# A transformer layer on one Trainium2 core: the dilated heads are placed between the NSA heads, and the order's estimate counts transfers and the port that VectorE and GpSimd share

## Chip, cores and metric

The kernel runs on one core of a Trainium2 chip. The metric is device time in microseconds (us) for one execution of the whole layer. Before the change it is 1748.33 us, the median of three runs (1747.14, 1748.33 and 1748.94 us).

## What is computed

One decoder layer on 1024 tokens of width 1024, in float32: a normalisation, one input projection, three causal token mixers side by side, a gated merge, a residual, and a gated feed-forward network with a short convolution. Cut to what matters here:

```python
h = rms_norm(x, norm1_g)
proj = h @ w_in + b_in                      # 6166 columns: q, k, v of all heads, and 3 x 1024 gate columns
y_a = fox_attention(qa, ka, va, fa)         # 4 heads, full causal, a decay per head
y_b = dilated_attention(qb, kb, vb, ...)    # 6 heads in 3 groups, strides 1, 4, 16; outputs weighted by their
                                            # softmax denominators
y_c = nsa_attention(qc, ...)                # 6 heads in 2 groups; each head has three parts:
#   scores against 63 compressed keys -> probabilities p_c and, summed over the group's three heads, an importance
#   of 16 blocks of 64 tokens; the 8 best blocks are selected for each query
#   "selected" attention over those blocks, and "window" attention over the last 512 tokens
g = sigmoid(gates).reshape(1024, 3, 1024)
merged = g[:, 0] * (y_a @ w_pa) + g[:, 1] * (y_b @ w_pb) + g[:, 2] * (y_c @ w_pc)
x = x + merged @ w_o
x = x + conv_ffn(rms_norm(x, norm2_g), ...)
out = rms_norm(x, final_g)
```

The compressed scores of a group must be known before its selected heads can start; its window heads do not need them. The 24 gate blocks (128 gate columns each, numbered 0 to 23) are needed only in the merge.

## The kernel before, in words

**Arithmetic.** Every float32 operand is split into a high and a low float32r part: ScalarE (ACT) casts the high part and VectorE (DVE) or GpSimd (POOL) subtracts to get the low one. A product is then three matmuls on TensorE (PE): high by high, high by low, low by high (`mm3`, L285 to L287).

**Stages.** (1) Normalisation, transposes, the first token projection, gate blocks 0 and 1, and the sums of tokens that the next stage needs (`token_sums`, L473 to L490). Gate blocks 0 and 1 are made by `gate` (L1436): a tile `f4` is filled by ACT in two halves, and each half is stored by a transfer on ACT's queue (L1440). The tag `f4` has two buffers, and `token_sums` takes its working tiles from the same two. (2) `proj_pairs` (L545 on) makes two blocks of 128 output columns at a time from seven half-size products in place of eight, 84 matmuls of 512 columns for a pair; 18 blocks of q, k and v and then the gate blocks 18 to 23 (`PAIRED = 18`), twelve pairs. (3) The compressed keys and values. (4) Attention, about 400 to 866 us in the trace. (5) Loads of the three mixers' outputs (`branch`, L1514 to L1519), the gate blocks that are left, and the merge. (6) Output projection. (7) Feed-forward network. The feed-forward and everything behind attention is not edited.

**Attention's order.** Attention is written as generators (one for each head, each strip of scores, each transpose, each product, each split). `Flow` runs them against an estimate: a queue for each of PE, DVE, ACT and POOL, a cost in us and a level for each request. When an engine is free in the estimate, the request of the lowest level is emitted. So `Flow` sets the program order on PE, DVE and ACT, and with it the order in which SyncE (SP) issues the transfers; on the chip each engine then works through its own list in that order. `yield "DVE", 1, 0.66, f` asks for DVE for 0.66 us at level 1. `F.move(kb)` is the estimate of a transfer, at 200 GB/s after all transfers that were already counted.

**What a head does.** `strips` computes the scores of two rows of 128 queries (L805 to L809, PE, level 2); `soften` takes the row maximum (DVE, L833) and the exponential (ACT, L841); the factors 1/sum follow (DVE, L850 to L853); `norm` multiplies the probabilities by them, on DVE (L864) or ACT (L865), whichever is free first in the estimate. The probabilities are transposed on PE (L907, level 1) into one of three PSUM banks X0 to X2, split by ACT (L923) and DVE (L926), and multiplied with the values (L953, L954, level 0). ACT and DVE take the result out (L970, L974) and SP stores it (L979). q, k and v tiles have two buffers each; a head's loads are issued when a buffer of its kind comes free.

**The order of the heads before.** A table `ORDER` of four kinds: f is a FoX head, d a dilated head, w a window head, n a selected head, and s, one for each NSA group, is the compressed scores of its three heads (L1329 to L1332, then DVE L1352 to L1377) and the selection (`nsa_rows`, L1391 to L1421). An s loads the q tiles of all three heads only for this. The w and n heads load them again.

**The filler.** Gate blocks from 3 up are made during attention by `fill`, one matmul at a time at level 9 (L1465): a block is 48 matmuls of 512 columns in two halves of 24, which sit in the banks X0 to X2 as well. The next block's weights are split meanwhile (`next_split`: ACT L1489, then one POOL instruction over 128x1024, L1493). `gate_out` adds the bias on ACT (L1476) into the tile `f4`, [128, 1024], one buffer in this stage, and SP stores each half (L1479). Thirteen blocks, 3 to 15, are filled; 16 and 17 are made behind attention, where `branch` loads too.

Of the kernel before, what the change touches and what calls it, by code (L numbers as in the profile page):

```python
# [6 lines left out]
F32 = mybir.dt.float32  # L7
# [8 lines left out]
P = 128  # L16
S = 1024
# [124 lines left out]
class Flow:  # L142
# [7 lines left out]
    def __init__(self):  # L150
        self.now, self.moved, self.n, self.events = 0.0, 0.0, 0, []
# [7 lines left out]
        self.groups, self.turned = r(), r()  # L159
# [14 lines left out]
    def step(self, g, value):  # L174
# [16 lines left out]
        else:  # L191

            taken = []
            for e, level, cost, emit, *lat in ask if isinstance(ask, list) else [ask]:
                self.n += 1
                heapq.heappush(self.queues[e], (level, self.n, cost, emit, lat[0] if lat else self.LAT[e], g, taken))
# [6 lines left out]
    def run(self):  # L203
        while True:
            while self.events and self.events[0][0] <= self.now + 1e-9:
                heapq.heappop(self.events)[2]()
            for e, q in self.queues.items():
                while q and q[0][6]:
                    heapq.heappop(q)
                if q and self.free[e] <= self.now + 1e-9:  # L210
                    _, _, cost, emit, lat, g, taken = heapq.heappop(q)
                    taken.append(e)
                    out = emit()
                    self.free[e] = self.now + cost
                    self.at(self.free[e] + lat, lambda g=g, out=out: self.step(g, out))
                    self.at(self.free[e], lambda: None)
# [5 lines left out]
class Trunk:  # L222
    def __init__(self, tc, a, taps=None):
# [4 lines left out]
        self.psA, self.steps = None, None  # L228

# [138 lines left out]
    def constants2(self):  # L368
# [39 lines left out]
        self.k2c = t([114, 256], F32R, "k2c")  # L408
# [131 lines left out]
    PAIRED = 18  # L540
# [280 lines left out]
    def soften(self, pair, part, ps, bank, place):  # L821
# [33 lines left out]
        yield "DVE", 0, 0.26 if pair.gates is None else 0.39, factors  # L855
# [5 lines left out]
    def norm(self, pair, x, left):  # L861
        nc, F = self.nc, self.F
        p, f, n = pair.blocks[x], pair.sm[:, 6 + x:7 + x], (pair.rows[x][2] - pair.rows[x][1] + 1) * P
        yield [("DVE", 1, 0.13 + n * 0.47e-3, lambda: nc.vector.tensor_scalar(p, p, f, None, ALU.mult)),  # L864
               ("ACT", 3, 0.16 + n * 0.85e-3, lambda: nc.scalar.mul(p, p, f))]  # L865
# [132 lines left out]
    def attention(self):  # L998
# [20 lines left out]
        def free(kind, n=1):  # L1019
# [10 lines left out]
                "s": lambda g: [head(set(), [lambda h=h: self.load_q(c, h, 6 + h)])[0] for h in range(3 * g, 3 * g + 3)],  # L1030
# [50 lines left out]
        pcs = {}  # L1081

        def select(g):
            pcs[g] = yield from self.nsa_select(g, heads["s", g], lambda: free("q"))

        def group_head(kind, h):
# [3 lines left out]
            k, v = heads[kind, 3 * g][1:]  # L1090
            vc = self.Box(t=self.vcs[g, 0 if r == 0 else 1], ready=Mark())
            vc.ready.on = True
            c0 = 0 if r == 0 else (r - 1) * 64
            for ip in range(4):
# [12 lines left out]
                if kind == "n":  # L1107
                    pc, ready = pcs[g]
                    self.t_step(u, [[(x, lambda i=i, c0=c0: pc[:, i, c0:c0 + P]) for x, i in enumerate((a, b))]],
# [984 lines left out]
```

## Time and profile before

| what | value |
|---|---|
| runs | 1747.14, 1748.33, 1748.94 us |
| the profiled execution's own time | 1745.82 us |
| its span, first to last instruction | 1744.1 us, 24501 instructions |
| mean clock granted to TensorE | 0.988 |
| PE busy | 1661.0 us (95%) |
| DVE busy | 1313.2 us (75%) |
| ACT busy | 830.5 us (48%) |
| POOL busy | 469.1 us (27%) |
| transfers | 275 MB, 158 GB/s on average |

The profiled execution is 2.5 us below the median of the runs. A busy PE in this profile is not PE at its peak: matmuls are pipelined, so that a 512-column matmul is shown with 0.39 us while the next one starts after 0.23 us. Times on the left of a row of the timeline are us from the span's start; what stands in square brackets behind a row is how long the engine had been idle before it, and what it had waited for.

### The profile page before, as it was taken

How to read it: one execution, taken by the hardware profiler on the slowest of the kernel's cores; microseconds unless marked ns; L12 is line 12 of the kernel's file. 1: busy time of each engine (PE TensorE's matmuls, PEld its weight loads, DVE VectorE, ACT ScalarE, POOL GpSimd, SP SyncE). 2: the span in 40 equal slices, each digit the busy share in tenths (PEclk: the TensorE clock that was granted, in tenths of full speed). 3: DMA queues.
4: the chain of work that ended last, by engine and by line, in shares of the span. 5: the costliest groups of instructions: out<-in, count | busy, mean ns of one | idle time of the engine just before them, and what ended most of it. 6: DMA issues, size and time to landing. Idle time of an engine off the chain costs nothing.

```text
span 1744.1 us, 24501 instructions
## 1 busy us (share of the span) xinstructions
PE 1661.0 (95%) x8468; PEld 1379.2 (79%) x8468; DVE 1313.2 (75%) x2230; ACT 830.5 (48%) x1599; POOL 469.1 (27%) x332
## 2 busy tenths in 40 slices
PE   6889999999989899999989999899999999999998
PEld 6678888877878688888877788688887888888876
DVE  8846776565886799888467617999999999866764
ACT  5323443235846378878555413433333343454451
POOL 3742322211010000000114320655546544200000
PEclk9999999999998999999999999999999999999999
DMA  6445566377776665332176710144545454487661
GB/s 205 119 128 145 151 167 167 122 177 184 199 209 175 171 203 160 101 112 64 54 256 203 269 49 13 37 163 157 188 149 195 163 170 157 140 269 230 213 228 51
DMA packets 228267, 275.08 MB, mean 158 GB/s; under 512 B 21412, under 2 KB 162314, under 8 KB 227934
## 3 DMA queue, kind: packets, MB, share of 16 engines
q1 hardware_dynamic: 224958, 265.48, 50.7%
q10 hardware_dynamic: 2736, 5.24, 0.8%
q0 software_dynamic: 448, 2.78, 0.5%
q8 instruction: 67, 1.10, 0.3%
q14 instruction: 58, 0.48, 0.1%
HBM read 194.23 MB, written 81.93 MB: 158 GB/s over the span
## 4 chain that ended last, share of the span: by engine, by line
PE 57%; DVE 20%; DMA 7%; issue 6%; ACT 5%; POOL 4%; SPq 0%; POOLq 0%; DVEq 0%; ACTq 0%
PE X L1465 6%; PE dn L287 5%; PE dn L285 5%; PE dn L286 5%; PE S L286 4%; PE S L287 4%; PE S L285 4%; PE X L907 3%; PE T L287 3%; DVE t L1730 3%; PE T L286 3%; PE T L285 3%; PE PV L954 2%; PE S L809 2%; DVE u L1788 2%
## 5 line engine op out<-in xcount | busy, mean ns | idle before, releaser
L926 DVE TENSOR_TENSOR tl<-X,th 128x512 fp32r<-128x512 f32 (+2 forms) x202 | 116.5, 586 | 24.9 <-ACT th L923 22.9
L1493 POOL TENSOR_TENSOR wl<-wr,wh 128x1024 fp32r<-128x1024 f32 x13 | 31.1, 2389 | 347.2 <-ACT wh L1489 314.0
L923 ACT CAST th<-X 128x512 fp32r<-128x512 f32 (+2 forms) x202 | 101.1, 507 | 39.6 <-PE X L907 36.0
L907 PE MATMUL X<-ident,p 128*128 128x128 f32 x610 | 99.4, 278 | 4.4 <-DVE tl L926 1.7
L833 DVE TENSOR_REDUCE sm<-S 128x1 f32<-128x640 f32 (+7 forms) x128 | 87.7, 711 | 20.0 <-PE S L809 19.7
L1730 DVE SCALAR_TENSOR_TENSOR t<-u,ccols,t 128x511 f32<-128x511 f32 (+1 forms) x88 | 96.7, 1099 | 7.5 <-ACT t L1725 6.4
L841 ACT ACTIVATE p<-S,sm 128x640 f32<-128x640 f32 (+7 forms) x128 | 90.9, 715 | 16.6 <-DVE sm L833 15.9
L953 PE MATMUL PV<-th,v 128*128 128x256 f32 (+1 forms) x362 | 94.6, 283 | 0.7 <-DVE y L974 0.7
L809 PE MATMUL S<-k,q 98*128 98x128 f32 (+6 forms) x240 | 91.7, 390 | 3.5 <-DMA q<-dq_c 2.5
L954 PE MATMUL PV<-tl,v 128*128 128x256 f32 (+1 forms) x362 | 90.0, 282 | 1.9 <-DVE tl L926 1.8
L805 PE MATMUL S<-k,q 128*128 128x512 f32 (+2 forms) x240 | 83.0, 346 | 7.1 <-ACT p L841 7.1
L1465 PE MATMUL X<-hTh,wl 128*128 128x512 f32 x208 | 86.5, 416 | 0.0
L1465 PE MATMUL X<-hTl,wh 128*128 128x512 f32 x208 | 86.3, 415 | 0.0
L1465 PE MATMUL X<-hTh,wh 128*128 128x512 f32 x208 | 85.5, 411 | 0.4 <-ACT f L1476 0.4
L907 PEld LDWEIGHTS X<-ident,p 128*128 128x128 f32 x610 | 70.9, 142 | 13.9 <-DVE tl L926 3.2
L263 POOL TENSOR_TENSOR wl<-wr,wh 128x384 fp32r<-128x384 f32 (+2 forms) x31 | 44.2, 1425 | 126.2 <-ACT wh L261 92.6
L954 PEld LDWEIGHTS PV<-tl,v 128*128 128x128 f32 x362 | 69.2, 191 | 6.7 <-DVE tl L926 3.2
L953 PEld LDWEIGHTS PV<-th,v 128*128 128x128 f32 x362 | 69.2, 191 | 3.6 <-ACT th L923 1.1
L1655 POOL TENSOR_TENSOR su<-wr 128x512 f32<-128x512 f32 x20 | 31.0, 1549 | 144.5 <-DMA wr<-w_up 71.3
L285 PE MATMUL dn<-hTh,wh 128*128 128x512 f32 x148 | 60.0, 405 | 10.2 <-ACT f L1436 10.2
L1731 ACT ACTIVATE t<-t 128x512 f32<-128x512 f32 x44 | 27.9, 633 | 82.6 <-DVE t L1730 82.6
L287 PE MATMUL dn<-blk,wh 128*128 128x512 f32 x152 | 60.4, 398 | 1.9 <-POOL wh L1667 1.0
(815 smaller groups left out, 5568.7 us busy)
## 6 DMA issues: line engine op xcount, KB each, us to landing
wr<-w_up SPq DMA_DIRECT2D x66, 256.0 KB
gr<-dg SPq DMA_DIRECT2D x24, 512.0 KB
t<-w_down SPq DMA_DIRECT2D x22, 512.0 KB
dt<-t SPq DMA_DIRECT2D x22, 512.0 KB
wr<-w_in SPq DMA_DIRECT2D x20, 512.0 KB
wr<-dl SPq DMA_DIRECT2D x39, 256.0 KB
wr<-w_in SPq DMA_DIRECT2D x36, 256.0 KB
q<-dq_c SPq DMA_DIRECT2D x18, 512.0 KB
```

Source lines behind the costliest of these rows:

```text
L285: nc.tensor.matmul(out, st[0], mv[0], start=first, stop=False)
L286: nc.tensor.matmul(out, st[0], mv[1], start=False, stop=False)
L287: nc.tensor.matmul(out, st[1], mv[0], start=False, stop=last)
L809: nc.tensor.matmul(out, q.t[1][0:R, qs], k.t[1][0:R, cs], start=False, stop=True)
L841: nc.scalar.activation(o.rearrange("p a b -> p (a b)"), u, AF.Exp, bias=mx[:, x:x + 1], accum_out=sm[:, 2 + x:3 + x])
L907: nc.tensor.transpose(ps[:, n * P:(n + 1) * P], b(), self.ident)
L923: nc.scalar.copy(g.th[:, cs], ps[:, cs])
L926: yield "DVE", 0, 0.07 + cs.stop * 1.04e-3, lambda: nc.vector.tensor_tensor(g.tl[:, cs], ps[:, cs], g.th[:, cs].bitcast(F32), ALU.subtract)
L953: nc.tensor.matmul(unit.pv[:, oc], w, g.th[:, cs], start=first and i == 0, stop=False)
L954: nc.tensor.matmul(unit.pv[:, oc], w, g.tl[:, cs], start=False, stop=e)
L1465: nc.tensor.matmul(p, w[i][:, k], self.hT[hh][j][:, k], start=x == 0, stop=x == 23)
L1730: nc.vector.scalar_tensor_tensor(o, i, cw[2 - sh], o, ALU.mult, ALU.add)
```

## The change

It has six parts.

1. **The order of the heads.** The kind s is gone. `nsa_select` is called at the start of each window head, with that head's own q tile, for its two halves; after the group's third window head the selection `nsa_rows` runs. `ORDER` has 22 heads in place of 24, and the six dilated heads stand between the NSA heads of group 0 (w0 d0 w1 d1 w2 d2 n0 d3 n1 d4 n2 d5), the FoX heads 1 to 3 between the window heads of group 1 (w3 f1 w4 f2 w5 f3), and n3 n4 n5 at the end as before. The second part of the compressed keys `k2c` has 98 rows in place of 114, since a window head's q tile has no rows for the selection; those rows were zero.
2. **The shared port in the estimate.** Requests are now either `DVE` or `DVE*`; `DVE*` (the factors, `norm`, the sums of the compressed scores, the selection, the dilated merge) and `POOL` do not run at the same time in the estimate. A request that waits for the port is passed over by others. Some costs were changed (`norm`, the selection).
3. **Splits in pieces.** The POOL instruction L1493 over 128x1024 becomes four over 128x256, with 0.65 us each in the estimate.
4. **Transfers in the estimate.** The stores of gate blocks and the loads of their weights are counted with `F.move`. The weights' load is issued before that wait rather than 2 us after the split.
5. **The gate tile.** `f4`, [128, 1024], becomes two tiles of [128, 512], `f0` and `f1`, in attention and behind it, taken in turn by each half; a half's tile comes free in the estimate when its store has landed. In the first stage both halves take a tile of 512 from the tag `f4`.
6. **Eight gate blocks in pairs.** `PAIRED` is 16: the blocks 16 to 23 are made in pairs, thirteen pairs in all; `fill` makes 3 to 13; 14 and 15 are made behind attention.

From L285 on, line numbers are 12 to 15 higher in the new code, and from L1326 on 5 to 15 higher.

```diff
@@ class Flow
+        self.f, self.groups, self.turned = r("f0", "f1"), r(), r()
...
+                port, e = e in ("DVE*", "POOL"), e.rstrip("*")
+                heapq.heappush(self.queues[e], (level, self.n, cost, emit, lat[0] if lat else self.LAT[e], g, taken, port))
...
+                ready = [o for o in q if not o[6] and not (o[7] and self.port > self.now + 1e-9)]
...
+                op = min(ready, key=lambda o: o[:2])
...
+                if port:
+                    self.port = self.free[e]
@@ proj_pairs
-    PAIRED = 18
+    PAIRED = 16
@@ norm
-        yield [("DVE", 1, 0.13 + n * 0.47e-3, lambda: nc.vector.tensor_scalar(p, p, f, None, ALU.mult)),
-               ("ACT", 3, 0.16 + n * 0.85e-3, lambda: nc.scalar.mul(p, p, f))]
+        yield [("DVE*", 1, 0.13 + n * 0.5e-3, lambda: nc.vector.tensor_scalar(p, p, f, None, ALU.mult)),
+               ("ACT", 3, 0.2 + n * 0.85e-3, lambda: nc.scalar.mul(p, p, f))]
@@ attention
-                "s": lambda g: [head(set(), [lambda h=h: self.load_q(c, h, 6 + h)])[0] for h in range(3 * g, 3 * g + 3)],
...
+            if kind == "w":
+                if r == 0:
+                    sels[g] = self.Box(pc=self.ap.tile([P, NT, 192], F32, "pc"), done=Mark(),
+                                       imp=self.ap.tile([P, 4, 64], F32, "imp"))
+                    sels[g].done.on = True
+                yield from self.nsa_select(g, r, q, sels[g])
+                if r == 2:
+                    F.proc(self.nsa_rows(g, sels[g]))
...
-    ORDER = (("f", 0), ("d", 0), ("d", 1), ("f", 1), ("d", 2), ("d", 3), ("s", 0), ("f", 2), ("d", 4), ("d", 5),
...
+    ORDER = (("f", 0), ("w", 0), ("d", 0), ("w", 1), ("d", 1), ("w", 2), ("d", 2), ("n", 0), ("d", 3), ("n", 1), ("d", 4),
...
@@ gate
-        gt = self.st.tile([P, S], F32, "f4")
...
+            gt = self.st.tile([P, 512], F32, self.gate_tags[hh])
@@ fill
-        for f in range(3, self.PAIRED):
+        for f in range(3, self.PAIRED - 2):
...
-            F.proc(self.next_split())
+            if self.wloaded:
+                F.proc(self.next_split())
@@ gate_out
+        place = yield F.f
+
+        def out():
+            gt = self.ap.tile([P, 512], F32, place)
+            nc.scalar.activation(gt, ps, AF.Identity, bias=self.cols[:, 20 + f:21 + f])
+            return gt
+
+        gt = yield "ACT", 0, 0.6, out
         F.dn.give(bank)
         yield 0.1
-        nc.sync.dma_start(self.dg[f][:, cs], gt[:, cs])
+        nc.sync.dma_start(self.dg[f][:, cs], gt)
+        yield F.move(256)
+        F.f.give(place)
@@ next_split
-        yield "POOL", 0, 2.4, low
+        for k in range(0, 8, 2):
+            yield "POOL", 0, 0.65, lambda k=k: low(k), 0.0 if k < 6 else F.LAT["POOL"]
         mark.set(F)
-        yield 2.0
         self.load_w()
+        yield F.move(512)
```

Three places in the programs show what moves. The first is SP's queue where the last loads before group 1 of the NSA heads are issued, before the change; `dg<-f` is the store of half a gate block, and what stands ahead of it are loads of q, k and v.

```order
L775 DMA v_5808<-dv_a_150 128x8x128
L754 DMA q_1049_5875<-dq_c_145 128x1024
L755 DMA q_1050_5876<-dq_c_145 64x1024
L758 DMA q_1050_5876<-dax_30_135 34x1024
L766 DMA k_1051_5880<-dk_w_149 64x1024
L767 DMA k_1051_5880<-dk_w_149 64x1024
L768 DMA k_1052_5881<-dk_w_149 64x1024
L770 DMA k_1052_5881<-day_141 34x1024
L775 DMA v_5886<-dv_w_153 128x8x128
L1479 DMA dg_165<-f_1031_5754 128x512
```

This is the same queue in the changed program where the keys of the second window group are loaded.

```order
L991 DMA dyb_59_164<-y_1211_6533 64x256
L770 DMA q_1223_6579<-dax_33_138 34x1024
L787 DMA v_6576<-dv_b_151 128x8x128
L778 DMA k_1224_6583<-dk_w_149 64x1024
L779 DMA k_1224_6583<-dk_w_149 64x1024
L780 DMA k_1225_6584<-dk_w_149 64x1024
L782 DMA k_1225_6584<-day_141 34x1024
L991 DMA dyb_59_164<-y_1216_6555 64x256
L1489 DMA dg_165<-f_1229_6611 128x512
```

Before, two values tiles, a q and a k stand in one block ahead of the gate's store; now the loads of q, v and k are spread between stores of outputs.

The second place is DVE in the compressed scores of the first group, before the change: `csm` and `ce` are the sums and the exponentials, `imp` the importance, `pc` the probabilities.

```order
L1352 TENSOR_REDUCE csm_4902<-S_845_4843 128x4
L1353 TENSOR_SCALAR csm_4902<-csm_4902 128x4
L1354 TENSOR_TENSOR ce_4901<-S_845_4843,csm_4902 128x256
L1363 TENSOR_REDUCE csm_4902<-ce_4901 128x4
L1364 TENSOR_SCALAR csm_4902<-csm_4902 128x4
L1365 RECIPROCAL csm_4902<-csm_4902 128x4
L1372 TENSOR_TENSOR imp_4748<-ce_4901,csm_4902 128x256
L1373 TENSOR_TENSOR pc_4747<-imp_4748,gsig_396 128x4x64
L974 TENSOR_TENSOR y_858_4931<-PV_4908,y_858_4931 64x256
L1352 TENSOR_REDUCE csm_4955<-S_853_4888 128x4
```

And this is the same second half of a head's compressed scores in the changed program, inside the window head 0.

```order
L1357 TENSOR_REDUCE csm_4014<-S_639_3952 128x4
L1358 TENSOR_SCALAR csm_4014<-csm_4014 128x4
L1359 TENSOR_TENSOR ce_4013<-S_639_3952,csm_4014 128x256
L938 TENSOR_TENSOR tl_650_4011<-X_646_3996,th_649_4010 128x512
L986 TENSOR_TENSOR y_654_4028<-PV_3975,y_654_4028 64x256
L1368 TENSOR_REDUCE csm_4014<-ce_4013 128x4
L1369 TENSOR_SCALAR csm_4014<-csm_4014 128x4
L1370 RECIPROCAL csm_4014<-csm_4014 128x4
L1377 TENSOR_TENSOR imp_3898<-ce_4013,csm_4014 128x256
L1378 TENSOR_TENSOR pc_3897<-imp_3898,gsig_396 128x4x64
L938 TENSOR_TENSOR tl_658_4042<-X_653_4023,th_657_4041 128x512
```

The wait of DVE for ACT's exponential, between `ce` and the next `csm`, now has other heads' splits (`tl`) and outputs (`y`) in it, and the next head's compressed scores no longer follow at once.

The third place is ACT in the first stage, around the second half of gate block 0, before the change. `f_149` is a working tile of the token sums, `f_150` the gate tile, and `T3h` and `T4h` are casts of the sums.

```order
L588 CAST wh_899<-wr_893 128x512
L1436 ACTIVATE f_150_696<-dn_748,cols_364 128x512
L588 CAST wl_902<-wr_893 128x512
L1440 DMA dg_165<-f_150_696 128x512
L473 CAST T4h_476<-sl_775 128x512
L473 CAST T3h_474<-f_149_690 128x512
L473 CAST T4h_476<-f_149_690 128x512
L1436 ACTIVATE f_168_811<-dn_812,cols_364 128x512
```

Here is the same place in the changed program, where `f_159` is the second half's own tile.

```order
L600 CAST wh_901<-wr_895 128x512
L485 CAST T3h_474<-f_149_690 128x512
L485 CAST T4h_476<-f_149_690 128x512
L1441 ACTIVATE f_159_773<-dn_748,cols_364 128x512
L485 CAST T4h_476<-sl_776 128x512
L1445 DMA dg_165<-f_159_773 128x512
L600 CAST wl_904<-wr_895 128x512
L1441 ACTIVATE f_170_837<-dn_812,cols_364 128x512
```

Two casts of `f_149` have moved ahead of the gate's second half.

More of the change, by code (lines that the diff above doesn't have):

```diff
@@ L207, in run @@
             for e, q in self.queues.items():
[L208 to L216, printed above, removed]
+                if not q or self.free[e] > self.now + 1e-9:
+                    continue
+                ready = [o for o in q if not o[6] and not (o[7] and self.port > self.now + 1e-9)]
+                q[:] = [o for o in q if not o[6]]
+                heapq.heapify(q)
+                if not ready:
+                    continue
+                op = min(ready, key=lambda o: o[:2])
+                q.remove(op)
+                heapq.heapify(q)
+                _, _, cost, emit, lat, g, taken, port = op
+                taken.append(e)
+                out = emit()
+                self.free[e] = self.now + cost
+                if port:
+                    self.port = self.free[e]
+                self.at(self.free[e] + lat, lambda g=g, out=out: self.step(g, out))
+                self.at(self.free[e], lambda: None)
             if not self.events:
@@ L1079, in dil_head @@
             free("k")
-        pcs = {}
-        def select(g):
-            pcs[g] = yield from self.nsa_select(g, heads["s", g], lambda: free("q"))
+        sels = {}
         def group_head(kind, h):
@@ L1186, in below @@
                 nc.vector.tensor_tensor(ln[:, g], ln[:, g], mx, ALU.subtract)
-        yield "DVE", 3, 0.7, below
+        yield "DVE*", 3, 0.7, below
         yield "ACT", 3, 1.5, lambda: nc.scalar.activation(ln, ln, AF.Exp)
@@ L1377, in rest, with nsa_rows @@
                 nc.vector.tensor_tensor(pd, e, bc(gt), ALU.mult)
-        yield "DVE", 1, 1.4 + 0.6 * half, rest
+        yield "DVE*", 1, 1.4 + 0.6 * half, rest
         F.ce.give()
         done.set(F)
-    def nsa_rows(self, g, imp, before):
-        nc, ap, F = self.nc, self.ap, self.F
-        yield before
+    def nsa_rows(self, g, sel):
+        nc, ap, F, imp = self.nc, self.ap, self.F, sel.imp
+        yield sel.done
         def select():
@@ L1991, in run @@
         gp = Pool(self, "gp", {"gr": 3, "acc": 2})
-        self.st = Pool(self, "last", {"gr": 3, "f4": 2}, side="right")
+        self.st = Pool(self, "last", {"gr": 3, "f0": 2, "f1": 2}, side="right")
         ys = {}
```

100 lines of the change are left out of this document (43 added, 57 removed).

## The prediction

> **What bounds the kernel now.** The windows of the attention stage come first, since most of the edits lie there: length, then the busy time (and instructions) of PE, PE's weight loads, DVE, ACT and POOL, then TensorE's granted clock, the transfers' share and GB/s.
>
> ```profile
> 400.00:866.00 466.00, 442.44 (x2921) 376.24 (x2921) 365.96 (x935) 322.23 (x776) 34.35 (x19) 0.98 0.54 146
> 400.00:480.00 80.00, 77.83 (x516) 65.98 (x516) 56.36 (x146) 57.47 (x148) 7.55 (x5) 1.00 0.73 183
> 480.00:620.00 140.00, 124.69 (x760) 105.31 (x759) 104.69 (x312) 72.82 (x191) 14.34 (x8) 0.93 0.70 186
> 620.00:840.00 220.00, 213.92 (x1491) 182.14 (x1490) 195.10 (x459) 179.53 (x416) 10.00 (x5) 1.00 0.41 120
> 480.00:500.00 20.00, 17.41 (x120) 15.39 (x118) 14.95 (x42) 12.48 (x37) 2.36 (x1) 0.91 0.68 185
> 540.00:560.00 20.00, 17.52 (x114) 16.19 (x112) 11.98 (x39) 12.78 (x47) 0.95 (x1) 0.83 0.53 166
> 600.00:620.00 20.00, 20.00 (x115) 16.62 (x115) 17.08 (x43) 14.85 (x35) 1.97 (x1) 0.87 0.54 121
> ```
>
> PE bounds the stage, but not evenly. It is idle for 466.0 - 442.4 = 23.6 us, and a clock of 0.98 costs another 0.02 x 466 = 9.3 us: 33 us are lost. Of the idle time 140.0 - 124.7 = 15.3 us lie between 480 and 620, where the compressed scores of both groups stand, and there the clock is 0.93. Between 620 and 840, with window and selected heads alone, PE is idle for 6.1 us of 220 (2.8%) at full clock, although DVE is busy there for 89%. So the chip can run this mix with DVE nearly full and PE almost always fed.
>
> The timeline of PE, DVE, POOL, SP and ACT then says what the idle time waits for; the bracket is the idle time before a row.
>
> ```profile
> 494.70 0.41 PE L907 MATMUL X<-ident,p 128*128 128x128 f32 x2 [1.62 <-DVE p L864]
> 522.65 0.60 PE L1408 MATMUL X<-ident,s 128*16 128x128 f32 x4 [2.15 <-DVE s L1398]
> 548.89 0.30 PE L809 MATMUL S<-k,q 98*128 98x128 f32 x1 [2.48 <-DMA q<-dq_c]
> 592.73 0.60 PE L1408 MATMUL X<-ident,s 128*16 128x128 f32 x4 [2.43 <-DVE s L1398]
> 599.58 0.79 PE L805 MATMUL S<-k,q 128*128 128x512 f32 x1 [5.32 <-ACT p L841]
> 622.86 0.39 PE L954 MATMUL PV<-tl,v 128*128 128x256 f32 x1 [1.13 <-DVE tl L926]
> 765.23 0.66 PE L907 MATMUL X<-ident,p 128*128 128x128 f32 x4 [1.68 <-DVE tl L926]
> ...
> 518.28 2.44 DVE L1394 TENSOR_TENSOR sc<-sc,sab 128x64 f32<-128x64 f32 x1
> 761.39 3.19 DVE L864 TENSOR_SCALAR p<-p,sm 128x640 f32<-128x640 f32 x2
> ...
> 518.25 2.39 POOL L1493 TENSOR_TENSOR wl<-wr,wh 128x1024 fp32r<-128x1024 f32 x1 [11.17 <-ACT wh L1489]
> 761.37 2.40 POOL L1493 TENSOR_TENSOR wl<-wr,wh 128x1024 fp32r<-128x1024 f32 x1 [44.51 <-ACT wh L1489]
> ...
> 584.92 6.20 SPq L1479 DMA_DIRECT2D dg<-f  x1
> 598.03 0.69 ACT L1476 ACTIVATE f<-X,cols 128x512 f32<-128x512 f32 x1 [12.30 <-DMA dg<-f]
> ```
>
> Three causes can be read. The longest gap, 5.32 us, belongs to the single gate tile: SP took 6.2 us to issue the store behind a run of q, k and v loads, ACT stood 12.3 us at L1476 until the tile was free, and the exponentials behind it on ACT's list came late. The gap of 2.48 us is a late q. The others are the port: a DVE instruction over 128x64 took 2.44 us beside a POOL split of 2.39 us, and the same happens at 761; PE's gaps of 1.62, 2.15, 1.13 and 1.68 us follow such collisions, 6.6 us in all.
>
> **The change, part by part.**
>
> *One more pair, two filled blocks fewer.* The copy of a pair's first product (L617) appears once in a pair, twelve times; the first and the last row give the period, and one row of the chain of waits gives the price of a filled block of 48 matmuls. A wait of a store stands before the last row, on ACT; PE was busy throughout.
>
> ```profile
> 119.26 0.59 ACT L617 COPY p<-dn 128x512 f32<-128x512 f32 x1 [0.75 <-PE dn L287]
> ...
> 333.58 0.59 ACT L617 COPY p<-S 128x512 f32<-128x512 f32 x1 [2.10 <-DMA dg<-u]
> ...
> 401.45 10.98 PE X L1465 x48
> ```
>
> A pair costs (333.58 - 119.26) / 11 = 19.5 us, all on the path. Two blocks of filler cost 2 x 10.98 = 22.0 us, and attention is bound by PE, so they come off it. Net -2.5 us. If PE did not bound attention any more, their removal would be worth nothing and the pair would be a loss of 19.5 us; that is a rival below.
>
> *The first stage.* PE's gaps around the two gate blocks and the second token projection are these; the two rows of ACT are the gate's second half and the cast that moves ahead of it, those of POOL two steps of the token sums.
>
> ```profile
> 74.90 0.79 PE L285 MATMUL dn<-hTh,wh 128*128 128x512 f32 x1 [5.73 <-ACT f L1436]
> 84.66 0.39 PE L285 MATMUL dn<-bh,hTh 128*128 128x274 f32 x1 [1.81 <-ACT f L1436]
> 98.68 0.39 PE L285 MATMUL dn<-bh,hTh 128*128 128x274 f32 x1 [3.46 <-DVE tm L680]
> ...
> 74.17 0.68 ACT L1436 ACTIVATE f<-dn,cols 128x512 f32<-128x512 f32 x1
> 83.40 0.62 ACT L473 CAST T4h<-f 128x512 fp32r<-128x512 f32 x1 [2.22 <-POOL f L489]
> 70.88 1.71 POOL L487 TENSOR_TENSOR sl<-hTh,sh 128x512 f32<-128x512 f32 x1
> 78.22 1.76 POOL L487 TENSOR_TENSOR f<-hTh,f 128x512 f32<-128x512 f32 x1 [2.90 <-DMA dg<-f]
> ```
>
> Now the working tile `f` waits until both halves of gate block 0 are stored (POOL at 78.22). In the changed order it needs only the first half's store, so it can follow POOL's step at 70.88 directly, at 72.6, 5.6 us earlier; but ACT takes its two casts before the gate's second half. The casts would end at about 83.40 + 0.62 - 5.6 = 78.4 and the second half follow there instead of at 74.2, so the gap of 5.73 grows by about 4 us; the 1.81 behind it and most of the 3.46 should go, and what follows starts earlier, since the next round of sums begins 5.6 us earlier and `tm` on DVE, on which PE waits at 98.68, stands behind it. An estimate from these rows is -2.5 us, with 0 and -4 as ends.
>
> *The compressed scores inside the window heads.* No computation is added: as many instructions on PE, DVE and ACT, and six q loads fewer. What goes is the run of six compressed scores in a row, a chain from DVE to ACT and back in which only the filler keeps PE busy, and the q loads of heads that only this run used. *The gate tile in halves* gives ACT a second tile, so that a store may take the time of a whole half more before ACT stands. *Pieces and the estimate of the port*: the loss at one collision is at most a piece, which costs 2.39 / 4 = 0.6 us by the row above, in place of 2.4. There are four pieces for a block and eleven blocks, 44 instructions in place of 12 or 13; the order avoids collisions only where the chip keeps to the estimate.
>
> What is lost afterwards is the largest unknown, and no row of before shows it. From one side it is bounded by the 33 us of now (the order may move the gaps and remove none), from the other by the part of 620 to 840 that is not a collision, (6.1 - 1.13 - 1.68) / 220 = 1.5%. The work of PE without gaps and at full clock is 466 - 33 - 22 = 411 us: at 1.5% that is 6 us. I take the whole share of 620 to 840, 2.8% of 411 = 11.4 us, and 3.6 us for the clock, two windows like the one at 480 (20 x 0.09 each): 15 us. The mix is the nearest one: DVE's 366 us, less 9 us for four collisions of about 2.2, over 411 + 15 us make 84%, and 620 to 840 ran with 89%. So -18 us, with ends of -27 and 0.
>
> How the clock falls matters for the 3.6 us. In the windows it stood at 0.91 at 480 and at 0.83 at 540, where the gaps were 1.62 and 2.48 us. The Trainium skill, in "TensorE: Matmul & The Clock Gate", Part 1, says that the clock halves only after an idle window of about 3.4 us. This trace differs: shorter gaps were followed by a slower clock. By the page, short gaps would cost no clock, and the sum would be 3.6 us lower.
>
> *Behind attention.* Two blocks are made there as before. SP issues the loads of `branch` behind the last filler's store in both orders, so the gap before the second of these blocks, 3.39 us, stays.
>
> ```profile
> 884.66 0.50 PE L285 MATMUL dn<-hTh,wh 128*128 128x512 f32 x1 [3.39 <-ACT f L1436]
> ```
>
> **The sum** is -2.5 - 2.5 - 18 = -23 us against the profiled execution's 1745.8 us, 1722.8 us. That execution is 2.5 us below the median of the runs, so the forecast for the median is 1725 us.
>
> **The rivals.**
>
> *The pieces do not help.* The chip drifts from the estimate within a few heads. A POOL piece waits for DVE too, and the next block's weights come after four such waits instead of one; POOL's pieces then collide as often as now and the filler is late when a gap needs it. For it: a split that starts a microsecond early or late meets another DVE instruction than the estimate had in mind. Against it: POOL was busy for 34 of 466 us, and a block's split can begin when the block before it begins. It would keep the 6.6 us of collisions and two more windows of clock like the one at 480, 3.6 us: 1725 + 10 = 1735 us.
>
> *Late transfers take the place of the gaps.* The NSA group holds one of two k and one of two v buffers for three heads, so each dilated head's k can only be loaded when the dilated head before it is done, during one window head. A late load costs what the one at 548.89 cost: 2.48 us, and 0.17 x 20 = 3.4 us of clock behind it, 5.9 us. There are nine such changes in the two interleaved groups. Against it: a head between them gives such a load about 18 us (the twelve window and selected heads take the 220 us from 620 on), and the six q loads that go make transfers lighter. If three or four of nine are late, the 18 us are gone: 1746 us, no change that can be measured.
>
> *DVE sets the pace: slower.* With two blocks fewer there is less filler to cover DVE's chains. If DVE reaches only the share that it has now over the whole stage, 366 / 466 = 78.5%, attention takes (366 - 9) / 0.785 = 455 us in place of 466. That is 11 us less against 19.5 more for the pair, and 2.5 less in the first stage: +6, 1754 us. It decides as soon as DVE's share stays under 79.5% (357 / 0.795 = 449; the 17 us saved there and the first stage just pay for the pair). Against it: the 89% of 620 to 840.
>
> **How the numbers follow.** Forecast 0.64, rival of the pieces 0.15, late transfers 0.12, DVE 0.09. About 0.2%, 3.5 us, is what a measurement of this kernel can tell from no change. The forecast and the first rival lie wholly on the faster side (0.79); of the late transfers a quarter is still faster (0.03), the rest within 0.2% (0.09); of the DVE case 0.01 is within 0.2%, the rest slower (0.08). So 0.82, 0.10 and 0.08. The forecast's own range goes from 1725 - 9 - 1.5 - 2.5 = 1712 (gaps of 6 us at full clock, the first stage at -4, and runs that lie no higher than the profiled execution) to 1734 with half of the 18 us; the range reaches on over the rival of the pieces to the edge of the late transfers, 1712 to 1745.
>
> **What would show it.** In the changed kernel's trace: 13 copies L629 (now L617) at 19.5 us; 528 filler matmuls in place of 624; attention's PE idle and slow clock near 15 us in place of 33, and the stage some 40 us shorter (466 - 22 - 18); no ACT wait of 12 us at the gate's bias; no DVE instruction of 128x64 over 1 us in the selection; the gap at 74.90 grown, the one at 98.68 shrunk. The forecast is wrong if gaps at the first scores of dilated heads name a DMA, or if PE's gaps name DVE between all heads while DVE's share stays near 79%.

## The result and the profile after

The changed kernel takes 1717.98 us, the median of four runs (1716.85 to 1719.81), beside 1747.74 us for the kernel before, measured with it. The medians differ by 29.8 us; the ratio is 0.9839, with a 95% interval of 0.9811 to 0.9866, so the kernel is 1.6% faster. The forecast was 1725 us in a range of 1712 to 1745. The profiled execution has a span of 1717.0 us, 27.1 us less than the 1744.1 of before. The other 2.7 us of the medians' difference lie in which execution was profiled: 1.9 us below its median before, 0.9 us above it now.

The stages come first, cut at the same events in both programs: the first pair's copy, the first filler matmul, the end of attention's last matmul, and 95 us of what follows. The columns are those of the prediction's windows: the stretch and its length, the busy time of PE, PE's weight loads, DVE, ACT and POOL with the number of instructions, the granted clock, the transfers' share and GB/s. Before:

```profile
0.00:119.26 119.26, 91.02 (x564) 82.26 (x565) 84.51 (x163) 49.65 (x97) 65.72 (x62) 0.96 0.51 151
119.26:401.26 282.00, 276.28 (x1273) 228.67 (x1271) 187.00 (x264) 105.65 (x168) 82.56 (x58) 1.00 0.59 158
401.26:864.95 463.69, 440.65 (x2912) 374.88 (x2912) 365.53 (x934) 321.18 (x775) 34.28 (x18) 0.98 0.54 146
864.95:960.00 95.05, 87.29 (x367) 68.83 (x367) 60.08 (x73) 47.49 (x63) 29.36 (x22) 0.98 0.68 225
```

And after:

```profile
0.00:117.31 117.31, 89.46 (x564) 81.25 (x565) 88.75 (x163) 49.66 (x98) 65.86 (x62) 0.96 0.51 153
117.31:418.34 301.03, 295.66 (x1356) 244.48 (x1355) 194.64 (x278) 110.89 (x176) 90.38 (x65) 1.00 0.58 155
418.34:837.60 419.26, 412.44 (x2815) 349.89 (x2814) 352.40 (x924) 322.57 (x779) 35.11 (x46) 1.00 0.54 142
837.60:932.90 95.30, 89.03 (x377) 69.61 (x378) 64.19 (x77) 49.53 (x65) 29.20 (x23) 1.00 0.70 232
```

First stage -1.95 us, pairs +19.0, attention -44.4, behind it +0.2: together -27.1. In attention PE now idles for 419.26 - 412.44 = 6.8 us and its clock is 1.00; before it was 23.0 us and 0.98. DVE is busy for 352.4 / 419.3 = 84%.

The three windows that the prediction showed at 480, 540 and 600 us read like this in the changed kernel, though other heads run in them now; all run at full clock, and PE is busy for 58.2 of the 60 us, where it was 54.9:

```profile
480.00:500.00 20.00, 19.82 (x134) 16.14 (x134) 18.19 (x50) 15.66 (x40) 2.98 (x4) 1.00 0.56 158
540.00:560.00 20.00, 18.43 (x125) 15.46 (x123) 17.45 (x49) 16.06 (x42) 0.00 (x0) 1.00 0.88 209
600.00:620.00 20.00, 20.00 (x138) 16.91 (x136) 16.57 (x46) 17.59 (x43) 2.82 (x4) 1.00 0.70 171
```

PE's timeline after, with every gap over 0.8 us from 70 us to the merge, without the pairs and the compressed keys:

```profile
78.74 0.80 PE L297 MATMUL dn<-hTh,wh 128*128 128x512 f32 x1 [9.57 <-ACT f L1441]
98.24 0.39 PE L297 MATMUL dn<-bh,hTh 128*128 128x274 f32 x1 [2.28 <-DVE tm L692]
433.44 0.50 PE L817 MATMUL S<-k,q 128*128 128x512 f32 x1 [1.04 <-ACT p L853]
558.20 0.30 PE L821 MATMUL S<-k,q 98*128 98x128 f32 x1 [1.49 <-issue]
764.01 0.63 PE L919 MATMUL X<-ident,p 128*128 128x128 f32 x4 [0.83 <-DVE tl L938]
839.14 0.50 PE L297 MATMUL dn<-hTh,wh 128*128 128x512 f32 x1 [1.55 <-ACT f L1483]
```

Inside attention three gaps of over 0.8 us are left, none over 1.5 us. ACT's wait of 12.30 us for a gate store has no successor. The longest gap of the kernel, 9.57 us, is the first stage's, in front of gate block 1.

### The profile page after: what moved, and what is told of

Read it like the earlier page. It is cut to its first block, busy times and chain, and to the rows that moved or that the text cites. A ratio compares the mean times of both kernels' runs of the same rounds, so it can differ in the third digit from the quotient of the medians.

```text
span 1717.0 us, 24504 instructions
## 1 busy us (share of the span) xinstructions
PE 1651.3 (96%) x8456; PEld 1367.6 (80%) x8456; DVE 1312.1 (76%) x2234; ACT 837.5 (49%) x1611; POOL 477.3 (28%) x367
## 4 chain that ended last, share of the span: by engine, by line
PE 51%; DVE 25%; issue 8%; DMA 7%; ACT 4%; POOL 4%; SPq 1%; POOLq 0%; DVEq 0%; ACTq 0%
PE X L1470 5%; PE dn L297 4%; PE dn L298 4%; PE dn L299 4%; DVE t L1744 4%; PE X L919 3%; PE S L298 3%; PE S L299 3%; PE S L297 3%; DVE u L1802 3%; PE T L299 2%; PE T L298 2%; PE T L297 2%; PE PV L966 2%; PE S L821 2%
## 5 line engine op out<-in xcount | busy, mean ns | idle before, releaser
L1506 POOL TENSOR_TENSOR wl<-wr,wh 128x256 fp32r<-128x256 f32 x44 | 32.5, 771 | 311.9 <-ACT wh L1501 297.2
L853 ACT ACTIVATE p<-S,sm 128x640 f32<-128x640 f32 (+7 forms) x128 | 90.8, 714 | 14.6 <-DVE sm L845 13.9
L1470 PE MATMUL X<-hTh,wh 128*128 128x512 f32 x176 | 73.1, 415 | 0.0
L1470 PE MATMUL X<-hTh,wl 128*128 128x512 f32 x176 | 72.6, 413 | 0.0
L1470 PE MATMUL X<-hTl,wh 128*128 128x512 f32 x176 | 71.8, 408 | 0.0
L1739 ACT ACTIVATE t<-u,ccols 128x512 f32<-128x512 f32 x44 | 36.0, 817 | 52.2 <-DVE u L1802 49.0
```

The costliest lines, as they stand in the source:

```text
L853: nc.scalar.activation(o.rearrange("p a b -> p (a b)"), u, AF.Exp, bias=mx[:, x:x + 1], accum_out=sm[:, 2 + x:3 + x])
L1470: nc.tensor.matmul(p, w[i][:, k], self.hT[hh][j][:, k], start=x == 0, stop=x == 23)
```

## The experiments

My theory of the gain was that three causes, each removed by its own edit, made the gaps: the gate store, the port and the late q. The rival was that the order of the heads, which spreads DVE's work and the loads, had removed all of them. Each ratio in the table is to the kernel before, run beside it. Attention's length, between the same events, is the finer measure: the same attention program took 419.26, 418.96, 418.50 and 418.19 us in four profiles, while all that lies behind it took between 875 and 882 us in profiles that make two gate blocks there. It still rests on one profile of each kernel.

| kernel | attention, us | PE idle in it | clock | ratio to before, 95% interval |
|---|---|---|---|---|
| changed kernel | 419.3 | 6.8 | 1.00 | 0.9839 [0.9811, 0.9866] |
| changed kernel, again | 419.0 | 6.3 | 1.00 | 0.9847 [0.9820, 0.9874] |
| one gate tile | 417.9 | 5.3 | 1.00 | 0.9856 [0.9832, 0.9881] |
| one POOL piece | 418.7 | 7.4 | 1.00 | 0.9865 [0.9845, 0.9886] |
| no port in the estimate | 419.7 | 8.9 | 1.00 | 0.9868 [0.9845, 0.9890] |
| tile, pieces, port and costs undone | 423.6 | 10.8 | 0.99 | 0.9856 [0.9835, 0.9878] |
| compressed scores in runs | 422.2 | 9.7 | 0.99 | 0.9864 [0.9837, 0.9891] |
| old order of heads | 451.4 | 23.4 | 0.97 | 1.0028 [1.0013, 1.0044] |
| before, new order alone (12 filled blocks) | 440.6 | 13.3 | 0.98 | 0.9896 [0.9857, 0.9936] |
| before, eight gates in pairs alone | 442.0 | 26.3 | 0.99 | 0.9996 [0.9974, 1.0019] |
| changed kernel, ten gates in pairs | 406.9 | 14.6 | 1.00 | 0.9864 [0.9836, 0.9891] |

### One gate tile

```diff
-        place = yield F.f
...
-            gt = self.ap.tile([P, 512], F32, place)
...
+                if gt is None:
+                    gt = self.ap.tile([P, S], F32, "f4")
```

> The changed kernel, with the filler's gate rows again in one tile of 128x1024 that the estimate does not know (attention alone; the gate block before it uses a whole tile too). Theory of three causes (store, port, late q; each edit removes its own): a store behind loads on SP holds ACT again at least once, as in the kernel before (gap 5.32 us and a slower clock behind it), so attention grows from 419 to 425 to 428 us and the whole by 6 to 9 us. Rival (the order alone spread the work and the loads, tile and port hardly matter): no run of loads is in front of a store any more, attention 419 to 421 us, the whole within 2 us.

Attention took 417.9 us: the rival's figure. SP's queue shows why. In the first 220 us of attention before, three rows of stores took long to issue, the last of them behind the loads that the listing of SP's queue ahead of the prediction shows:

```profile
407.73 5.76 SPq L1479 DMA_DIRECT2D dg<-f  x2
520.86 5.79 SPq L1479 DMA_DIRECT2D dg<-f  x1
584.92 6.20 SPq L1479 DMA_DIRECT2D dg<-f  x1
```

With the new order and the single tile only the first is left, and the next slowest of the stores in attention takes 0.55 us (the first row is two stores; it is left in the changed kernel too, as 4.82 us at 425.76):

```profile
427.64 5.51 SPq L1486 DMA_DIRECT2D dg<-f  x2
505.47 0.55 SPq L1486 DMA_DIRECT2D dg<-f  x1
```

A store that is issued in half a microsecond needs no second tile. The order is enough to remove the 12-us wait: in the kernel before with the new order alone (below), with its one tile, no instruction of ACT in attention waits for a store. It is not the only way: with the old order and all other edits (below) one store again took 5.11 us, at 544.72, and ACT waits for none either.

### One POOL piece, and no port in the estimate

```diff
...
-        for k in range(0, 8, 2):
-            yield "POOL", 0, 0.65, lambda k=k: low(k), 0.0 if k < 6 else F.LAT["POOL"]
+        yield "POOL", 0, 2.4, low
```

> The changed kernel, with POOL's split of a filled block in one instruction of 128x1024 again; the estimate keeps the port and costs it at 2.4 us. Theory of three causes: the estimate drifts by a microsecond or two, so three or four of eleven splits meet a DVE instruction, each about 1.6 us of PE (6.6 us for four in the kernel before): attention 424 to 427 us, the whole +5 to +8 us. Rival (order alone): 419 to 421 us.

```diff
-                port, e = e in ("DVE*", "POOL"), e.rstrip("*")
+                port, e = False, e.rstrip("*")
```

> The changed kernel with pieces, but the estimate knows no port: DVE's starred operations and POOL's pieces may be put at the same time. Theory of three causes: pieces alone bound a collision at 0.77 us, so of 44 pieces perhaps half hold a DVE instruction for some 0.4 us, 9 us of DVE, of which a third reaches PE: attention 421 to 424 us, the whole +2 to +5 us. Rival (order alone): within 2 us. If the pieces do nothing without the estimate: +8 us or more.

418.7 and 419.7 us: again the rival's figures. The whole times do not decide it: by the ratios the three kernels undone one at a time lie 2 to 5 us above the two measurements of the changed kernel, more than the rival's 2 us for some and within the theory's 2 to 5 us for the last, but each interval is some 4 us wide to either side. Collisions did come. With one piece PE has two gaps of the predicted size,

```profile
489.61 0.33 PE L919 MATMUL X<-ident,p 128*128 128x128 f32 x1 [1.46 <-ACT p L877]
566.52 0.55 PE L919 MATMUL X<-ident,p 128*128 128x128 f32 x3 [1.59 <-DVE tl L938]
```

but there are two where I expected three or four, and other small gaps are missing, so that PE's idle time is 7.4 us beside 6.8.

### The old order of heads

```diff
-    ORDER = (("f", 0), ("w", 0), ("d", 0), ("w", 1), ("d", 1), ("w", 2), ("d", 2), ("n", 0), ("d", 3), ("n", 1), ("d", 4),
-             ("n", 2), ("d", 5), ("w", 3), ("f", 1), ("w", 4), ("f", 2), ("w", 5), ("f", 3), ("n", 3), ("n", 4), ("n", 5))
+    ORDER = (("f", 0), ("d", 0), ("d", 1), ("f", 1), ("d", 2), ("d", 3), ("f", 2), ("d", 4), ("d", 5),
+             ("f", 3), ("w", 0), ("w", 1), ("w", 2), ("n", 0), ("n", 1), ("n", 2), ("w", 3), ("w", 4), ("w", 5),
+             ("n", 3), ("n", 4), ("n", 5))
```

> The changed kernel with the heads in the old order (forget and dilated heads first, the twelve window and selected heads last); the compressed scores stay in the window heads, the tiles, the pieces and the port too. Theory of three causes: the order itself is worth the late q and little else, but the selection's DVE work (about 38 us) now falls wholly into the back half, where DVE was busy for 89% already: attention 425 to 432 us, the whole +6 to +13 us. Rival (order alone made the gain): the 22 us come back, attention 440 us or more. A third reading, that the order does nothing: 419 to 421 us.

451.4 us, the rival's range: with all other edits in place the kernel is no faster than before. The windows of this run, front to back:

```profile
418.76:640.00 221.24, 219.03 (x1408) 185.23 (x1408) 154.46 (x418) 149.54 (x376) 28.21 (x38) 1.00 0.70 181
640.00:740.00 100.00, 97.48 (x667) 82.23 (x666) 87.58 (x224) 75.40 (x171) 8.20 (x9) 1.00 0.49 138
740.00:870.20 130.20, 111.56 (x744) 92.74 (x744) 112.95 (x300) 92.48 (x217) 0.00 (x0) 0.91 0.17 48
```

DVE is busy for 70% of the front and for 87% of the last 130 us, where PE idles for 18.6 us at a clock of 0.91. POOL has no split there, because the filler had run out:

```profile
712.31 0.40 PE L1471 MATMUL X<-hTh,wl 128*128 128x512 f32 x1
766.39 0.79 PE L817 MATMUL S<-k,q 128*128 128x512 f32 x1 [2.32 <-ACT p L853]
789.74 0.50 PE L817 MATMUL S<-k,q 128*128 128x512 f32 x1 [2.20 <-ACT p L853]
```

The first row is the last filler matmul, at 712 us; in the changed kernel it stands at 837 us, at attention's end. So the heads that lean on DVE ran last, and without cover. This is not the old program's order, though: there the compressed scores ran ahead of the window heads, here they stand in them and fall into the back half too. The kernel before with as many filled blocks (the pairs alone, below) has the old order with the scores ahead, and its attention takes 442.0 us:

```profile
740.00:864.12 124.12, 116.36 (x841) 100.34 (x841) 109.93 (x261) 100.31 (x233) 4.78 (x2) 1.00 0.27 76
```

DVE is as full there (89%), but the filler lasts to 825 us and PE idles for 7.8 us at full clock. Under the old order the other edits together thus cost 9.4 us of attention; which of them cost it, this run does not tell. The 32 us between 451.4 and 419.3 are the order's worth with the scores in the window heads, not its worth alone.

### The new order alone

The kernel before, with only its table changed; the two runs of compressed scores stand whole ahead of w0 and w3.

```diff
...
+    ORDER = (("f", 0), ("s", 0), ("w", 0), ("d", 0), ("w", 1), ("d", 1), ("w", 2), ("d", 2), ("n", 0), ("d", 3), ("n", 1), ("d", 4),
+             ("n", 2), ("d", 5), ("s", 1), ("w", 3), ("f", 1), ("w", 4), ("f", 2), ("w", 5), ("f", 3), ("n", 3), ("n", 4), ("n", 5))
```

> The kernel before with the new order of heads alone (the runs of compressed scores stay whole, each ahead of its group's first window head; one tile, one piece, no port, eighteen paired gates). Its estimate fills 12 blocks in place of 13, so one block (11 us) moves behind attention. Theory of three causes: the late q and some crowding of loads go, the tile and the port still cost: attention 463.7 - 11 - 6 to 9, so 444 to 447 us, the whole -6 to -9 us against the kernel before. Rival (order alone made the gain): attention 430 us, the whole -22 us.

440.6 us, between the theory's 444 to 447 and the rival's 430. A block is worth 10.8 us (next experiment), so with eleven blocks it would be 429.7 us. But this profiled execution, 1735.4 us, is the slowest of its four, the others 1723.3 to 1728.9; the ratio gives 18 us off the whole, 11 to 25. The order alone is thus worth from 12 us to most of the gain; the profile does not say where in the other executions the further microseconds went. The gap of 5.32 us is gone. What the order leaves stands in PE's timeline: the runs of compressed scores (L1331 and L1407) and the port (L907).

```profile
442.77 0.35 PE L1331 MATMUL S<-k2c,q 114*128 114x256 f32 x1 [1.37 <-DMA q<-dax]
461.29 0.61 PE L1407 MATMUL X<-ident,s 128*16 128x128 f32 x4 [1.89 <-DVE s L1397]
543.95 0.76 PE L907 MATMUL X<-ident,p 128*128 128x128 f32 x3 [1.61 <-DVE p L864]
630.02 0.39 PE L1331 MATMUL S<-k2c,q 114*128 114x256 f32 x1 [2.12 <-DMA q<-dax]
```

### The pairs alone, and one pair more

In the kernel before:

```diff
-    PAIRED = 18
+    PAIRED = 16
...
-        for f in range(3, self.PAIRED):
+        for f in range(3, self.PAIRED - 2):
```

> The kernel before with eight gates in pairs and eleven filled blocks, and nothing else of the change. Forecast's first term (attention is bound by PE, a filled block costs its 11 us): pairs +19.5, attention 463.7 - 22 = 441.7 us, the whole -2.5 us. Rival (the filler is the only cover of the runs of compressed scores, so its removal brings gaps): attention 450 to 463 us, the whole +6 to +19 us.

Attention went from 463.7 to 442.0 us, 21.7 us for two blocks, 10.8 each; the pairs took 300.7 us in place of 282.0. The forecast's term holds to 1 us, as a net: PE's busy time fell by 24.9 us, 3 us more than the two blocks' 22.0, and its idle time rose from 23.0 to 26.3 us. The whole did not move outside its interval (0.9974 to 1.0019), as -2.5 us would not. The gaps of before stayed, the 5.32 us one as 5.38:

```profile
540.93 0.88 PE L1408 MATMUL X<-ident,s 128*16 128x128 f32 x4 [2.21 <-DVE s L1398]
613.79 0.79 PE L805 MATMUL S<-k,q 128*128 128x512 f32 x1 [5.38 <-ACT p L841]
```

So the runs of compressed scores did not get worse by two blocks of filler fewer; what came in are three gaps of 0.9 to 1.4 us behind the last filler matmul (825 us), each waiting for DVE. In the changed kernel, two more blocks were moved:

```diff
-    PAIRED = 16
+    PAIRED = 14
```

> The changed kernel with ten gates in pairs and nine filled blocks. If PE still bounds attention: pairs +19.5, attention 419.3 - 22 = 397 us, the whole -2.5 us, with DVE at 352 / 397 = 89%. Rival (DVE's chains come through once the filler is thinner): attention stays above 405 us, the whole +5 to +19 us.

Attention became only 12.4 us shorter, where the pairs grew by 18.1. Up to 760 us PE is fed; then the filler is used up (its last matmul is at 780.81) and DVE is busy for 90% of the rest:

```profile
436.56:760.00 323.44, 319.03 (x2192) 270.40 (x2191) 276.02 (x756) 249.31 (x618) 29.32 (x38) 1.00 0.60 156
760.00:843.40 83.40, 73.21 (x529) 62.73 (x529) 75.15 (x169) 67.87 (x155) 2.37 (x1) 1.00 0.32 91
```

Ten of those 83 us are idle, and the whole is not faster (0.9864). Eleven filled blocks last to attention's end; nine do not. That is the point at which the third rival begins.

### Second theory: order, place of the scores, and the rest at once

After these runs I took the order for about half, and the place of the compressed scores for the other half. One kernel takes the scores out of the window heads into a run ahead of them,

```diff
-                yield from self.nsa_select(g, r, q, sels[g])
...
+            for r in range(3):
+                yield from self.nsa_select(g, r, heads["s", g][r], sels[g])
+                free("q")
```

> The changed kernel with the compressed scores of a group taken out of its three window heads and put in one run of six ahead of the first of them, with three q loads more for each group; order, tile halves, pieces and port as changed. Second theory (the order gives about half of the gain and the place of the scores the other half; tile, pieces and port give nothing that the order has not given already): gaps at the two runs come back, attention 427 to 431 us, the whole +8 to +12 us. Rival (the other half came from tile, pieces and port together, each of which covers for the others): attention 419 to 422 us, the whole within 3 us.

and one undoes the tile, the pieces, the port, and the costs and transfers in the estimate together.

> The changed kernel with the order and the compressed scores in the window heads, and the rest of attention as before at once: one gate tile unknown to the estimate, one split of 128x1024, no port and the old costs in the estimate. Second theory (order and place of the scores make the gain): attention 419 to 423 us, the whole within 4 us. Rival (tile, pieces and port cover for each other, so that each undone alone showed nothing): four collisions of 1.6 us and the store's 5 us with its slow clock are back, attention 428 to 433 us, the whole +9 to +14 us.

422.2 us and 423.6 us: both above the changed kernel, neither by as much as the reading that would make it the whole other half (427 us or more). Of the second theory the part on the scores failed, then, and of its rival the part on the rest. The whole times are 1722.45 and 1722.11 us beside 1720.36 for the changed kernel in the same session, some 2 us more, which lies inside the intervals. With the runs PE waits for q tiles that only the run needs, as before:

```profile
637.67 0.39 PE L1339 MATMUL S<-k1c,q 128*128 128x256 f32 x1 [2.88 <-DMA q<-dq_c]
640.66 0.58 PE L1342 MATMUL S<-k2c,q 98*128 98x256 f32 x1 [2.56 <-DMA q<-dax]
```

With tile, pieces and port undone, collisions are back. The three gaps are PE's; the row of DVE is a 128x2 instruction held for 2.34 us, and the row of POOL the split beside it:

```profile
488.35 0.91 PE L919 MATMUL X<-ident,p 128*128 128x128 f32 x3 [1.94 <-ACT p L877]
650.67 0.88 PE L919 MATMUL X<-ident,p 128*128 128x128 f32 x3 [1.99 <-DVE p L876]
735.63 0.81 PE L919 MATMUL X<-ident,p 128*128 128x128 f32 x3 [1.77 <-DVE p L876]
...
485.07 2.34 DVE L862 TENSOR_SCALAR sm<-sm 128x2 f32<-128x2 f32 x1
...
484.85 2.53 POOL L1500 TENSOR_TENSOR wl<-wr,wh 128x1024 fp32r<-128x1024 f32 x1 [51.06 <-DMA k<-dk_b]
```

That pieces and port cover for each other when one is undone alone would explain this; it is not shown, since no run undoes these two and nothing else. With eleven blocks throughout, a path from the old program to the new reads 442.0, then 429.7 with the order, 423.6 with the scores in the window heads, 419.3 with the rest: 12.3, 6.1 and 4.3 us. The path takes the scores ahead of the rest and rests on one profile a step. The first two shares depend on the one profiled execution of the order alone; by the whole times the order's share is larger and the scores' smaller.

### The first stage

The steps of the token sums, and so their casts on ACT, are placed behind the gate block's second half.

```diff
-                self.step(2)
...
         self.dense(evac)
+        if f != 2:
+            self.step(4)
```

> The changed kernel with the token sums' steps put behind a gate block's second half in the program, in place of behind its first half (first stage alone). If ACT's order is what holds PE at the gap of 9.57 us: the gap goes, and the first pair's copy comes 4 to 9 us earlier than 117.3 us, the whole -4 to -9 us. Rival (the sums set the end of the stage, PE only waits elsewhere): the gap moves to the token projection or the first pair, the copy within 1.5 us of 117.3.

> The changed kernel itself once more, as the mark for the run beside it: 1715 to 1720 us, and first pair's copy between 117 and 119.5 us, since the same first stage took 117.3 to 119.1 us in five profiles.

> The kernel of the first stage's experiment once more, with five rounds beside the changed kernel: if the 3 to 4 us that the first pair's copy came earlier stay to the end, 0.2% under the changed kernel; if they are given back behind it (pairs 1.4 us longer, the part behind attention 1.6 us longer in the first profile), no difference outside the interval.

The gap of 9.57 us did not go. It became 5.70 us in the first profile and 8.15 us in the second, and the first pair's copy came at 114.34 and 117.22 us, where 4 to 9 us were expected. The whole took 1718.88 us (ratio 0.9840, 0.9803 to 0.9877) and 1715.83 us (0.9825, 0.9801 to 0.9848), the second beside 1720.36 us (0.9847) for the changed kernel in the same session. The intervals overlap: a gain of up to some 4 us is possible and not shown. ACT's order is not all that holds PE there, for with the casts behind the second half a gap of 5.7 to 8.2 us stays. In the second profile ACT stood before that half for a step of DVE:

```profile
73.46 0.23 ACT L743 ACTIVATE fax<-fax 128x32 f32<-128x32 f32 x1 [3.80 <-DVE fax L742]
```

In the first it did not, and the gate's second half came at 74.17 us in place of 76.72.

## Why the prediction was right, and where it was not

**The pair and the two filled blocks** (-2.5 us): right in size and mechanism. The thirteen copies run from 117.31 to 351.08 us, 19.5 us apart, 528 filler matmuls are left, and in the pairs alone a block came off attention at 10.8 us.

**The first stage** (-2.5 us): right in size on the mean, half right in mechanism. The mean first copy of nine profiles with the changed first stage is 118.15 us, that of three with the old one, which spread from 119.26 to 121.35, is 120.63: -2.5. The front was as told: POOL's step on `f` follows at 72.39 (72.6 was forecast), the casts end at 78.1 (78.4), PE's gap grew by 3.8 us (about 4), and the one of 1.81 us is gone.

```profile
70.70 1.72 POOL L499 TENSOR_TENSOR sl<-hTh,sh 128x512 f32<-128x512 f32 x1
72.39 1.71 POOL L499 TENSOR_TENSOR f<-hTh,f 128x512 f32<-128x512 f32 x1
...
77.48 0.62 ACT L485 CAST T4h<-f 128x512 fp32r<-128x512 f32 x1 [2.18 <-POOL f L501]
78.00 0.68 ACT L1441 ACTIVATE f<-dn,cols 128x512 f32<-128x512 f32 x1
```

The back was not. Of the 3.46 us, most of which should have gone, 1.2 went, and PE's gaps of over 0.8 us from 70 us to the copy add up to 11.9 us in both profiles. The first matmul behind that gap came at 98.24 in place of 98.68 us; the other 1.5 us of the -1.95 lie behind it, where the same 137 matmuls, busy throughout, met another clock. Before and after:

```profile
98.68:119.26 20.58, 20.58 (x137) 19.73 (x138) 5.53 (x18) 4.59 (x10) 8.05 (x12) 0.92 0.43 123
98.24:117.31 19.07, 19.07 (x137) 18.22 (x138) 5.53 (x18) 4.59 (x11) 8.06 (x12) 1.00 0.47 132
```

In these two profiles that is luck, and no part of the forecast: of the nine profiles of the changed first stage five show 19.1 us there and four 20.5 to 20.6, and of the three old ones one shows 19.07. Up to this matmul the means differ by 2.1 us (98.42 and 100.55), and that much may be the edit's. The -2.5 was also no sum of its rows, since +4, -1.81 and most of -3.46 make about -1; the rest was put on an earlier start of what follows.

**What is lost in attention** (15 us left, so -18): the term that was mis-sized. 6.8 us were left, all of it idle and, to the two digits that the profile prints, none of it clock; that is the bound of 6 us that I had worked out from the quiet part of 620 to 840 and not taken. The share of DVE was as forecast, 84%. Not all of the smaller loss reached the time: PE's own work, put at 411 us in a window 2.3 us longer, took 412.4, so the 33 us of loss before were some 3 us too many. Their 9.3 us of clock came from a share of two digits. With -22.4 in place of -18 the sum is -27.

**Which edit removes which gap**: wrong. I gave the gap of 5.32 us to the single gate tile, and a large part of the rest to pieces and port. One gate tile under the new order loses nothing that attention shows; tile, pieces, port and costs together give 4 us. The traces of before showed what each gap waited for, and this was read rightly; but the waits were ends of chains, and with the new order alone the store's chain did not start: loads of several heads in a row ahead of a store. PE's waits for the q tiles of the compressed scores went only when the scores moved into the window heads. Whether the halves alone would have removed the 12-us wait under the old order wasn't tried; with the other edits beside them it was gone.

**Behind attention** (3.39 us stay): wrong in detail, and right as a sum by chance. In place of 3.39 us there is a gap of 1.55 us ahead of the first block and smaller ones later, and the 95 us behind attention are 0.2 us longer.

**The rivals.** Late transfers did not come: no gap names a DMA; the one of 1.49 us at 558.20, a first score, names no releaser and may be one. The first rival let POOL's pieces collide as often as the whole splits and kept 10 us of loss for it; the whole loss that is left in attention is 6.8 us, and no 128x2 instruction of DVE takes over 0.71 us. The third rival, DVE in front, did not come either, at a share of 84%. It comes when the old order is put back: the share is then 355 / 451 = 79%, the 78.5% that the rival assumed, and the kernel falls back to 1.0028 of before.

**The clock.** The Trainium skill, "TensorE: Matmul & The Clock Gate", Part 1, gives about 3.4 us of idleness for a fall to half, by a window that runs freely. The 9.57 us gap agrees; the granted clock behind it was 0.50:

```profile
78.70:83.00 4.30, 4.26 (x10) 3.39 (x11) 4.06 (x9) 1.70 (x3) 4.28 (x7) 0.50 0.71 216
```

But in the kernel with tile, pieces and port undone, gaps of 1.94 and 1.99 us were followed by these windows:

```profile
490.00:500.00 10.00, 10.00 (x73) 8.50 (x72) 9.05 (x24) 8.16 (x20) 0.00 (x0) 1.00 0.46 137
650.00:660.00 10.00, 9.32 (x55) 8.11 (x55) 7.01 (x20) 6.84 (x16) 0.27 (x1) 0.83 0.48 116
```

The one cost no clock, the other 0.17 of 10 us, in finer windows a clock of 0.50 to 0.52 for 3.3 us. So here gaps well under 3.4 us did cost clock, and the measurement decides. A gap of 2 us cost nothing in one place and nearly as much again as itself in the other; from these runs a forecast can only give it a mean.

## What to carry to other kernels

Where several engines share a stage, first look at how each engine's busy share lies over its length, and mix the parts that lean on the fuller engine with those that lean on the other, so that the filler lasts to the end; here that was worth more than the repairs of single waits together, and with the old order put back the kernel with all the other edits was no faster than before. A wait's releaser names the last link, and an edit made at that link is needed only if the chain ahead of it stays: undo each edit alone and then all together before it gets the credit. Work moved out of a stage as filler pays in full only as long as what stays still covers the stage to its end (in the changed kernel eleven blocks did, nine did not).

## What was not expected of the hardware

The same instructions in the first stage ended between 117.3 and 119.1 us in nine profiles of it. Most of that is the clock of one stretch: 137 matmuls without a gap took 19.1 us at 1.00 in five profiles and 20.5 to 20.6 us at 0.92 in four, and the idle gap just before did not sort them (2.2 to 2.6 us in the five, 2.0 to 3.1 in the four). One and the same program had its gate gap at 5.70 us in one execution and at 8.15 in another. So 2 us at one place of a single profile are no difference. A DVE instruction over 128x2, some 0.16 us in the median, took 2.34 us beside a POOL instruction of 2.53 us; in pieces of about 0.74 us the worst such instruction in attention took 0.71 us.
